# Second expert product: the last 64 tokens wholly from gathered rows, 192 dense tokens in five stationary sets

## The chip, the core and the metric

The kernel runs on one core of a Trainium2 chip. The metric is device time in microseconds; "before" is the median of three runs. TensorE (PE) multiplies matrices: a stationary operand of up to 128 columns is loaded (PEld), and a moving operand of up to 512 columns streams past it. VectorE (DVE), ScalarE (ACT) and GpSimd (POOL) work on 128 partitions; SyncE (SP) only starts DMA transfers here. Every engine takes its instructions in the order of the program; semaphores order the engines among each other.

## The reference

Two layers work on 256 tokens of 1024 numbers. Each layer first mixes tokens (convolution, windowed attention, spatial gating) and then runs PEER, a product-key retrieval over 16384 experts of one neuron each. Only PEER matters here:

```python
q = (t @ w_pq).reshape(T, PEER_HEADS, 2, PEER_HALF)
s = jnp.einsum('thpk,hpnk->thpn', q, sub_keys)
top_s, top_i = lax.top_k(s, PEER_TOPK)                 # 16 of 128 keys, twice per head
...
best_s, best_pos = lax.top_k(cand_s..., PEER_TOPK)     # 16 experts per head, 8 heads
gate = jax.nn.softmax(best_s, axis=-1)
act = jax.nn.gelu(einsum('td,thkd->thk', t, expert_down[experts]))
return einsum('thk,thkd->td', gate * act, expert_up[experts])
```

Each token so uses 128 of the 16384 experts. Scale and shift of the norms come from `c` by `w_ada`, 48 chunks of 128 outputs per layer ("modulation chunks").

## The kernel before

**First product.** `experts` computes the activations of all 16384 experts for all 256 tokens. The table `expert_down` comes in 128 chunks of 128 experts, 512 KB each, through five buffers `raw`. `cast_step` splits each chunk into a high half `hi` (ScalarE, L237) and a low half `lo` (VectorE, L230), with three buffers each, and `chunk_mm` makes 24 matmuls of 256 columns (8 row blocks by `hi x high`, `lo x high`, `hi x low`). GELU puts the result for a pair of chunks into `arena`.

**Gates.** `make_onehots` builds, for four tokens at a time, four one-hot matrices on GpSimd (L927) and three products on VectorE; `gate_mm` makes 8 small matmuls of them (L940, L941), whose result is the gate of every expert for these tokens. `gate_use` multiplies the activations of the chunks that are already there; `act_use` does it for later chunks. There are 64 such groups for 256 tokens; they are spread over the chunks from the end of the retrieval's work up to chunk 124 (`G_LAST`).

**Second product.** `combine` multiplies the gated activations, chunk by chunk, with `expert_up` (128 chunks of 128 experts by 1024 columns), under a hand-written order. `split(q)` makes high and low halves `hh` of four chunks' activations. A chunk has tokens 0 to 127 over 1024 columns and tokens 128 to 255 over `D - WIDE` columns, 768 in layer 0 and 640 in layer 1: 12 matmuls (L1037). Eight "whole" chunks per layer (`WHOLE_UP`) are multiplied unsplit in fp32; each of their matmuls runs as two.

**Gathered columns.** The last `WIDE` columns (256, 384) of the last 128 tokens come another way. During the first product SP copies these columns of `expert_up` into a DRAM tensor `rows`, and ScalarE's queue writes each pair's ungated activations of tokens 128 to 255 beside them. In the second product GpSimd gathers, for pick `k` of 128, one such row per token (token = partition) into a ring of eight buffers (`fetch`, L1017); VectorE takes the token's activation out of it by a product with the identity (L1023) and adds the weighted row to a sum (L1028, `add_row`). Row `k + 8` can be gathered when row `k` has been added. Rows are added between chunk 12 and chunk 125, about one per chunk, and each addition stands in VectorE's order between the low halves of the chunks, which run two chunks ahead.

**Modulation.** Layer 0's first product has 32 modulation chunks between its chunks, its second product 16, layer 1's first product 8. Each is a product with `c` and a sum on VectorE (L194), in two halves of 512 columns, with `c` in PSUM, in the first products.

At chunk 68 the second product loads `X` back from DRAM, and in layer 0 at chunk 72 `tables` loads three tables of the next layer by GpSimd's queue and masks one of them, for which GpSimd waits.

Of the kernel before, what the change touches and what calls it, by code (L numbers as in the profile page):

```python
# [9 lines left out]
F32 = mybir.dt.float32  # L10
# [7 lines left out]
P = 128  # L18
# [25 lines left out]
SPARSE = (True, True)  # L44
WIDE = (256, 384)
RING = 8
PICKS = 128
F_FIRST = 12
F_LAST = 125
WHOLE_UP = ((12, 24, 36, 48), (12, 24, 36, 48))  # L50
# [4 lines left out]
NG = S // 4  # L55
# [3 lines left out]
def hybrid_trunk(ctx: ExitStack, tc: tile.TileContext, x_in, c_in, vec_in, w_ada, w_in, w_out, w_pq,  # L59
# [34 lines left out]
    flat = arena.rearrange("p a b -> p (a b)")  # L94
    hh = consts.tile([P, 2, DC, S], F32R, name="hh")
    picks = consts.tile([P, S], F32, name="picks")
    parts = consts.tile([P, 3, S], F16, name="parts")
    chosen = consts.tile([P, 2, P], F32, name="chosen")
    c_dram = dram.tile([1, D], F32, name="c_dram")
    rows = {n: dram.tile([P * P, WIDE[n] + P], F32, name=f"rows{n}") for n in range(DEPTH) if SPARSE[n]}  # L100
# [38 lines left out]
    R_IX = region(0, 2, P)  # L139
    R_SUM = region(2 * S, max(WIDE))  # L140
# [22 lines left out]
    class Src:  # L163
        c = cact
# [24 lines left out]
    def ada_chunk(layer, col, raw):  # L189
        sides = Src.c if isinstance(Src.c, list) else [Src.c]  # L190
        w = D // len(sides)
        for k, (c, m) in enumerate(zip(sides, (mods[layer], halves))):
            v = raw[:, k * w:(k + 1) * w]
            op = nc.vector.scalar_tensor_tensor(v, v, 1.0, c, op0=OP.mult, op1=OP.mult, accum_out=m[:, col:col + 1])  # L194
            if len(sides) > 1 and k == 0:
                tc.keep_in_program_order(op)
        n = 8
        if layer == 0 and col < G1:
            n = 1
        if (col + 1) % n == 0:  # L200
            lo = col + 1 - n
            m = mods[layer][:, lo:lo + n]
            if len(sides) > 1:
                nc.vector.tensor_add(m, m, halves[:, lo:lo + n])
            nc.vector.tensor_add(m, m, vec[:, layer, V_ADA + lo:V_ADA + lo + n])
            if lo // 8 in (SC1 // 8, SC2 // 8):
                at = lo % 8 + (V_N1 if lo // 8 == SC1 // 8 else V_N2)
                nc.vector.scalar_tensor_tensor(m, m, 1.0, vec[:, layer, at:at + n], op0=OP.add, op1=OP.mult)

    def cast_step(late=None):  # L210
# [7 lines left out]
        if kind == "ada" and isinstance(Src.c, list):  # L218
# [5 lines left out]
        else:  # L224
# [20 lines left out]
            while Src.held:  # L245
                ada_chunk(*Src.held.pop(0))
# [12 lines left out]
    halves = consts.tile([P, 48], F32, name="halves")  # L259
    mods = [consts.tile([P, 48], F32, name=f"mod{i}") for i in range(DEPTH)]  # L260

    def ada(layer, groups):
        return [("ada", w_ada[layer, p], (layer, p)) for g in groups for p in range(8 * g, 8 * g + 8)]
# [15 lines left out]
    for layer in range(DEPTH):  # L279
# [16 lines left out]
        ups = [("whole" if n // 2 in WHOLE_UP[layer] else "mat", up[layer, n], None) for n in range(128)]  # L296
        if layer + 1 < DEPTH:
            dn = mix(dn, ada(0, [5]) + ada(1, range(3)), 24, 124)
            ups = mix(ups, ada(1, [3, 4]), 6, 120)
        else:  # L300
            dn = mix(dn, ada(1, [5]), 40, 120)
        seq += dn + ups
# [464 lines left out]
    def retrieval(layer, update, late):  # L767
# [80 lines left out]
        def to_picks(b):  # L848
# [4 lines left out]
            if b == 1 and SPARSE[layer]:  # L853
                nc.vector.scalar_tensor_tensor(chosen[:, 0, :], sel[:, 1, :], float(P), sel[:, 0, :], op0=OP.mult,
                                               op1=OP.add)
                nc.scalar.copy(chosen[:, 1, :], sel[:, 2, :])
            nc.vector.tensor_copy(picks[:, t], ps[:, 0:P])  # L857
# [57 lines left out]
    def experts(layer, rest):  # L915
# [28 lines left out]
        def gate_use(g, ps, done):  # L944
            v = ps.rearrange("p (t i) -> p i t", t=4)
            a = arena[:, :, 4 * g:4 * g + 4]
# [6 lines left out]
        def act(pair, ps, tdone):  # L953
            tmp = gelu(pair, ps, tdone)
            if SPARSE[layer]:
                i = 2 * pair
                ungated = work.tile([P, 2, P], F32, name="ungated", tag="ungated", bufs=1)
                nc.scalar.activation(ungated, ps.rearrange("p (i t) -> p i t", i=2)[:, :, P:], AF.Gelu)
                nc.scalar.dma_start(rows[layer].rearrange("(j i) c -> i j c", i=P)[:, i:i + 2, WIDE[layer]:], ungated)
                tc.keep_in_program_order(nc.sync.dma_start(  # L960
                    rows[layer][i * P:(i + 2) * P, :WIDE[layer]],
                    up[layer, i:i + 2, :, D - WIDE[layer]:].rearrange("j i c -> (j i) c")))
            return tmp

        def gelu(pair, ps, tdone):
            i = 2 * pair
            v = ps.rearrange("p (i t) -> p i t", i=2)
            if tdone < S:
                nc.scalar.activation(arena[:, i:i + 2, tdone:], v[:, :, tdone:], AF.Gelu)
            if tdone:  # L970
                tmp = work.tile([P, 2, S], F32, name="gt", tag="gt", bufs=1)
# [4 lines left out]
        def act_use(pair, tmp, tdone):  # L976
            if tmp is not None:
                i = 2 * pair
                a = arena[:, i:i + 2, :tdone]
                nc.vector.tensor_mul(a, a, tmp[:, :, :tdone])  # L980

        splits = {}

        def split(q):

            n = 2 if q == 0 or {2 * q, 2 * q + 1} & set(WHOLE_UP[layer]) else 4
            for i in range(4 * q, 4 * q + 4, n):
                src = arena[:, i:i + n, :]
                if i // 2 in WHOLE_UP[layer]:
                    hi, lo = src, None  # L990
                else:
                    slot = slice(i % 8, i % 8 + n)
                    hi, lo = hh[:, 0, slot, :S], hh[:, 1, slot, :S]
                    nc.scalar.copy(hi, src)
                    nc.vector.tensor_sub(lo, src, hi.bitcast(F32))  # L995
                for k in range(n):
                    splits[i + k] = hi[:, k, :], None if lo is None else lo[:, k, :]

        def combine(layer, late):


            qg = None
            sparse = SPARSE[layer]
            wide = WIDE[layer]
            dense = D - wide
            ring = region(4 * S, RING, wide + P)
            total = R_SUM[:, :wide]
            pieces = [(0, 0, 512), (0, 512, D)] + ([(1, 0, dense // 2), (1, dense // 2, dense)] if sparse else
                                                   [(1, 0, 512), (1, 512, D)])
            turns = [pieces[0], *pieces[2:], pieces[1]] if sparse else [pieces[0], pieces[2], pieces[1], pieces[3]]  # L1010
            acc = {p: bank("acc", 4) for p in turns}
            where, w8 = (R_IX[:, n, :] for n in range(2))
            fetched = added = 0

            def fetch(k):

                nc.gpsimd.indirect_dma_start(  # L1017
                    out=ring[:, k % RING, :], out_offset=None, in_=rows[layer][:, :],
                    in_offset=bass.IndirectOffsetOnAxis(ap=where[:, k:k + 1].bitcast(U32), axis=0))

            def add_row(k):
                v = ring[:, k % RING, :]
                nc.vector.scalar_tensor_tensor(v[:, wide:], v[:, wide:], chosen[:, 1, k:k + 1], ident, op0=OP.mult,  # L1023
                                               op1=OP.mult, accum_out=w8[:, k:k + 1])
                if k == 0:
                    nc.vector.tensor_scalar(total, v[:, :wide], w8[:, 0:1], None, op0=OP.mult)
                else:
                    nc.vector.scalar_tensor_tensor(total, v[:, :wide], w8[:, k:k + 1], total, op0=OP.mult, op1=OP.add)  # L1028

            if layer + 1 < DEPTH:  # L1030
                Src.c = work.tile([P, D], F32, name="cb", tag="oh", bufs=2)
                nc.gpsimd.dma_start(Src.c, bass.AP(tensor=c_dram.tensor, offset=c_dram.offset,
                                                   ap=[[0, P], [1, D]]))

            def add(i, piece, w, u, last=False):
                t, lo, hi = piece
                nc.tensor.matmul(acc[piece][:, :hi - lo], w[:, t * P:(t + 1) * P], u[:, lo:hi],  # L1037
# [224 lines left out]
```

## Time and profile before

| | |
|---|---|
| median of three runs | 1782.73 us (1777.23 to 1783.0) |
| profiled execution, its own time | 1781.52 us |
| its span in the trace | 1779.7 us |
| TensorE busy | 1728.6 us (97%) |
| VectorE busy | 1516.9 us (85%) |
| ScalarE busy | 916.7 us (52%) |
| GpSimd busy | 915.5 us (51%) |
| DMA | 493.36 MB, mean 277 GB/s |
| granted TensorE clock | 0.996 |

A layer's first product with its gates lies at about 205 to 594 us and 1085 to 1468 us, its second product at 594 to 912 and 1468 to 1774. The busy share of TensorE counts the modelled end of each matmul, which overlaps the next one; what TensorE really needs is seen from the distance of starts.

### The profile page before, as it was taken

Reading aid. Unit: us, or ns where it says so; the run is one execution under the profiler, and the core shown is the slowest. Engines: PE = TensorE matmul, PEld = TensorE weight load, DVE = VectorE, ACT = ScalarE, POOL = GpSimd, SP = SyncE. Lnnn points to the kernel's source line nnn. Section 1 sums busy time; section 2 is a strip of 40 time slices with the busy share of each in tenths; the row PEclk is TensorE's granted clock in tenths of the full one; section 3 lists DMA queues with packets and bytes.
Section 4 is the critical chain, followed back from the end, with each engine's and each line's share of the span. In section 5 each row is a group of like instructions: output and inputs, shape, how many; then the busy total and the mean of one; then the engine's idle time right before and its main releaser. Section 6 shows DMA issues by size and latency. Waiting matters only on the chain. (4 is left out here: it accounts for less than half of the span.)

```text
span 1779.7 us, 34446 instructions
## 1 busy us (share of the span) xinstructions
PE 1728.6 (97%) x12504; PEld 1595.0 (90%) x12504; DVE 1516.9 (85%) x3465; ACT 916.7 (52%) x1421; POOL 915.5 (51%) x827
## 2 busy tenths in 40 slices
PE   7999999999999999999999999999999999999998
PEld 6889999999999888888889899999999998888886
DVE  5868997789889689989987599958888878999998
ACT  2446455555445544444557565655555455444553
POOL 1000203679989267666600002128999964777672
PEclk9999999999999999999999999999999999999999
DMA  9965688888878899999964447988887778999995
GB/s 365 320 236 177 206 254 301 279 278 273 280 251 266 287 325 328 332 363 323 352 202 143 169 151 237 295 272 264 270 263 259 257 255 294 358 349 347 348 357 204
DMA packets 190011, 493.36 MB, mean 277 GB/s; under 512 B 19537, under 2 KB 85457, under 8 KB 188690
## 3 DMA queue, kind: packets, MB, share of 16 engines
q1 hardware_dynamic: 134752, 405.33, 67.3%
q0 software_dynamic: 20128, 68.96, 10.6%
q10 hardware_dynamic: 34962, 16.88, 3.2%
q8 instruction: 98, 1.61, 0.4%
q14 instruction: 71, 0.58, 0.1%
HBM read 471.16 MB, written 61.87 MB: 300 GB/s over the span
## 5 line engine op out<-in xcount | busy, mean ns | idle before, releaser
L237 ACT CAST hi<-raw 128x1024 fp32r<-128x1024 f32 x538 | 564.5, 1051 | 594.5 <-PE ch L314 242.2
L230 DVE TENSOR_TENSOR lo<-raw,hi 128x1024 fp32r<-128x1024 f32 x538 | 660.0, 1228 | 115.5 <-ACT hi L237 111.7
L313 PE MATMUL ch<-hh,lo 128*128 128x256 f32 x2336 | 652.9, 279 | 7.5 <-DVE lo L230 7.5
L312 PE MATMUL ch<-hh,hi 128*128 128x256 f32 x2336 | 658.2, 282 | 0.0
L314 PE MATMUL ch<-hh,hi 128*128 128x256 f32 x2336 | 649.9, 278 | 0.0
L927 POOL TENSOR_SCALAR oh<-iota,picks 128x128 f16<-128x128 f16 x512 | 502.6, 1000 | 212.2 <-DVE picks L857 105.1
L1017 POOL DMA_INDIRECT arena<-rows,arena x256 | 373.5, 1459 | 222.9 <-DVE arena L1028 111.8
L313 PEld LDWEIGHTS ch<-hh,lo 128*128 128x128 f32 x2336 | 441.4, 189 | 9.6 <-DVE lo L230 9.1
L312 PEld LDWEIGHTS ch<-hh,hi 128*128 128x128 f32 x2336 | 441.0, 189 | 0.3 <-issue 0.3
L314 PEld LDWEIGHTS ch<-hh,hi 128*128 128x128 f32 x2336 | 440.0, 188 | 0.0
L1037 PE MATMUL acc<-hi,hh 128*128 128x512 f32 (+2 forms) x1920 | 420.7, 360 | 5.4 <-DVE hh L995 2.7
L1037 PEld LDWEIGHTS acc<-hi,hh 128*128 128x128 f32 x1920 | 339.9, 188 | 52.6 <-DVE hh L995 7.0
L1037 PE MATMUL acc<-lo,hh 128*128 128x512 f32 x960 | 231.4, 361 | 2.9 <-DVE lo L230 2.8
L1037 PEld LDWEIGHTS acc<-lo,hh 128*128 128x128 f32 x960 | 173.1, 188 | 28.3 <-DVE lo L230 5.4
L1028 DVE SCALAR_TENSOR_TENSOR arena<-arena 128x256 f32<-128x256 f32 (+1 forms) x254 | 140.3, 552 | 9.1
L932 DVE TENSOR_TENSOR oh<-oh,parts 128x512 f16<-128x512 f16 x256 | 101.6, 439 | 0.0
L788 POOL CAST arena<-arena 128x512 f16<-128x512 uint32 x32 | 27.2, 865 | 141.7 <-DVE arena L777 113.2
L951 ACT ACTIVATE arena<-g 128x240 f32<-128x240 f32 (+35 forms) x128 | 41.5, 325 | 100.0 <-DVE arena L948 91.5
L194 DVE SCALAR_TENSOR_TENSOR raw<-raw,acc 128x512 f32<-128x512 f32 x80 | 54.4, 680 | 43.8 <-DMA raw<-in_w_ada 43.7
L1023 DVE SCALAR_TENSOR_TENSOR arena<-arena,chosen,ident 128x128 f32<-128x128 f32 x256 | 88.8, 347 | 0.0
L940 PE MATMUL g<-oh 128*128 128x128 f16 x512 | 74.8, 222 | 10.5 <-POOL oh L927 6.9
L752 POOL DMA_DIRECT2D arena<-in_keys x2 | 1.2, 578 | 150.1 <-issue 96.8
(233 smaller groups left out, 1840.5 us busy)
## 6 DMA issues: line engine op xcount, KB each, us to landing
raw<-in_down SPq DMA_DIRECT2D x256, 512.0 KB, 4.7
raw<-in_up SPq DMA_DIRECT2D x256, 512.0 KB, 5.3
raw<-in_w_ada SPq DMA_DIRECT2D x96, 512.0 KB, 4.8
rows<-in_up SPq DMA_DIRECT2D x64, 384.0 KB, 5.7
raw<-in_w_pq SPq DMA_DIRECT2D x32, 512.0 KB, 4.0
rows<-in_up SPq DMA_DIRECT2D x64, 256.0 KB, 5.4
rows<-ungated ACTq DMA_DIRECT2D x128, 128.0 KB, 4.7
raw<-in_w_in SPq DMA_DIRECT2D x26, 512.0 KB, 4.5
```

The lines of the kernel that those rows point to most:

```text
L230: nc.vector.tensor_sub(lo, raw, hi.bitcast(F32))
L237: nc.scalar.copy(hi, raw)
L312: nc.tensor.matmul(dst, hi[:, cols], k[0], start=start, stop=False, **kw)
L313: nc.tensor.matmul(dst, lo[:, cols], k[0], start=False, stop=False, **kw)
L314: nc.tensor.matmul(dst, hi[:, cols], k[1], start=False, stop=stop, **kw)
L927: nc.gpsimd.tensor_scalar(oh[:, i, :], iota, picks[:, t:t + 1], None, op0=OP.is_equal)
L932: nc.vector.tensor_tensor(og[j], on, wide(1 + j), op=OP.mult)
L940: nc.tensor.matmul(dst, oh[:, i, :], og[0][:, i // 2, :, i % 2], start=True, stop=False)
L1017: nc.gpsimd.indirect_dma_start(out=ring[:, k % RING, :], out_offset=None, in_=rows[layer][:, :], in_offset=bass.IndirectOffsetOnAxis(ap=wh ...
L1023: nc.vector.scalar_tensor_tensor(v[:, wide:], v[:, wide:], chosen[:, 1, k:k + 1], ident, op0=OP.mult, op1=OP.mult, accum_out=w8[:, k:k + 1])
L1028: nc.vector.scalar_tensor_tensor(total, v[:, :wide], w8[:, k:k + 1], total, op0=OP.mult, op1=OP.add)
L1037: nc.tensor.matmul(acc[piece][:, :hi - lo], w[:, t * P:(t + 1) * P], u[:, lo:hi], start=piece not in opened, stop=last, skip_group_check=True)
```

## The change

The first 192 tokens are now dense over all 1024 columns, and the last 64 come wholly from gathered rows.

- `T = 192`: the gates are made for 192 tokens, in 48 groups (`NG`). `acts` is the arena with 192 tokens per chunk.
- `split` keeps high and low halves of 192 tokens in `sides`, and a second copy of the high half of tokens 128 to 191 behind their low half. So one stationary set `w1` holds 64 low and 64 high columns. A chunk has five stationary uses: `w0h` and `w0l` with `uh`, `w1` with `uh`, `w0h` and `w1` with `ul`, each over two pieces of 512 columns, 10 matmuls. `fold` (two identities one above the other) adds the two halves at the end, in `turn`.
- No chunk of `expert_up` is whole any more: 16 more chunks are split by `cast_step`.
- For the last 64 tokens a partition stands for a token and half of its picks: `pairs` holds 64 picks for each of 128 partitions. `fetch` gathers rows of 1024 columns from `expert_up` itself, 64 per layer, into a ring of four. Nothing is copied to `rows` any more; only the ungated activations of 64 tokens go to `act_rows`, and they are gathered apart, 64 gathers of 64 columns, in groups of eight (`fetch_acts`). `weights` takes a group's activations out by `fold`, three VectorE instructions. Group `g + 2` uses the buffers of group `g` and is gathered after `weights(g)`.
- Layer 0's first product has all 48 modulation chunks, each as one product of 1024 columns with `c` in SBUF; the second product has none.
- Additions run from chunk 9 to 126; `X` is loaded at chunk 92, the tables at 84.

```diff
+T = 192
+TS = S - T
+RING = 4
+GROUP = 8
+F_FIRST = 9
+F_LAST = 126
...
+                nc.scalar.copy(hi, src)
+                nc.scalar.copy(slot[:, :, 2 * T:2 * T + TS], src[:, :, P:])
+                nc.vector.tensor_sub(lo, src, hi.bitcast(F32))
...
+            def fetch_acts(g):
...
+                for k in range(g * GROUP, (g + 1) * GROUP):
+                    nc.gpsimd.indirect_dma_start(
+                        out=R_ACTS[:, k % (2 * GROUP), :], out_offset=None, in_=act_rows[layer][:, :],
+                        in_offset=bass.IndirectOffsetOnAxis(ap=where_act[:, k:k + 1].bitcast(U32), axis=0))
...
+                nc.vector.tensor_tensor(v, v, fold[:, None, :].to_broadcast([P, GROUP, TS]), op=OP.mult)
+                nc.vector.tensor_reduce(w, v, op=OP.add, axis=AX.X)
+                nc.vector.tensor_mul(w, w, pairs[:, 1, g * GROUP:(g + 1) * GROUP])
...
+            while fetched < RING:
+                fetch(fetched)
+                fetched += 1
+            fetch_acts(0)
+            fetch_acts(1)
             for i in range(128):
                 if i % 4 == 2 and 4 < i < 124:
                     split(i // 4 + 1)
                 uh, ul = next_chunk()
...
+                while added < want(i):
+                    add_row(added)
+                    added += 1
+                    if fetched < TS:
+                        fetch(fetched)
                         fetched += 1
+                g = -(-want(i + 2) // GROUP) - 1
+                if i >= F_FIRST - 2 and g > -(-want(i + 1) // GROUP) - 1:
+                    weights(g)
+                    if 1 < g + 2 < TS // GROUP:
+                        fetch_acts(g + 2)
...
+                    for w in (w0h, w0l):
+                        for p in pieces[:2]:
+                            add(i, p, w, uh)
+                    for p in pieces[2:]:
+                        add(i, p, w1, uh)
                     for p in pieces:
+                        add(i, p, w1 if p[0] else w0h, ul)
```

GpSimd's order in the second product of layer 0, before (L1017 are the rows, L1078 is `X`, L462 to L467 are the tables):

```order
L927 TENSOR_SCALAR oh<-iota,picks 128x128 x256
L1032 DMA cb<-c_dram 128x1024
L1117 DMA cb<-c_dram 128x1024
L1017 DMA arena<-rows_99,arena 128x384 x73
L1078 DMA arena<-x_dram 128x2048
L1017 DMA arena<-rows_99,arena 128x384 x5
L462 DMA arena<-in_rel_bias 128x2048
```

and of the change (L1006 are rows of 1024 columns, L1013 the activations):

```order
L925 TENSOR_SCALAR oh<-iota,picks 128x128 x192
L1006 DMA arena<-in_up,arena 128x1024 x4
L1013 DMA arena<-act_rows_102,arena 128x64 x24
L1006 DMA arena<-in_up,arena 128x1024 x8
L1013 DMA arena<-act_rows_102,arena 128x64 x8
L1006 DMA arena<-in_up,arena 128x1024 x8
```

Three groups of activations now stand between row four and row five, and eight gathers ahead of every eight rows after that. Further on, the tables follow two rows behind the last group:

```order
L1013 DMA arena<-act_rows_102,arena 128x64 x8
L1006 DMA arena<-in_up,arena 128x1024 x2
L458 DMA arena<-in_rel_bias 128x2048
L459 DMA arena<-in_sgu_w 128x512
L460 DMA arena<-in_sgu_b 128x256
L461 AFFINE_SELECT arena<-arena 128x512
L463 MEMSET arena 128x2x2
L1006 DMA arena<-in_up,arena 128x1024 x4
```

VectorE's order at the first additions of layer 0, before (L230 are low halves, L194 a modulation chunk, L995 a split):

```order
L194 SCALAR_TENSOR_TENSOR raw,mod_108<-raw,cb 128x1024
L230 TENSOR_TENSOR lo<-raw,hi 128x1024
L1023 SCALAR_TENSOR_TENSOR arena<-arena,chosen,ident 128x128
L1026 TENSOR_SCALAR arena<-arena 128x256
L1023 SCALAR_TENSOR_TENSOR arena<-arena,chosen,ident 128x128
L1028 SCALAR_TENSOR_TENSOR arena<-arena 128x256
L230 TENSOR_TENSOR lo<-raw,hi 128x1024
L1023 SCALAR_TENSOR_TENSOR arena<-arena,chosen,ident 128x128
L1028 SCALAR_TENSOR_TENSOR arena<-arena 128x256
L995 TENSOR_TENSOR hh<-arena,hh 128x1024
```

and of the change (L229 are low halves, L1021 to L1023 the weights of a group, L1028 the first and L1030 every later addition, L989 a split):

```order
L229 TENSOR_TENSOR lo<-raw,hi 128x1024 x2
L1021 TENSOR_TENSOR arena<-arena,fold 128x512
L1022 TENSOR_REDUCE arena<-arena 128x8
L1023 TENSOR_TENSOR arena<-arena,pairs 128x8
L229 TENSOR_TENSOR lo<-raw,hi 128x1024 x2
L1028 TENSOR_SCALAR arena<-arena 128x1024
L989 TENSOR_TENSOR hh<-arena,hh 128x4x192
L229 TENSOR_TENSOR lo<-raw,hi 128x1024
L1030 SCALAR_TENSOR_TENSOR arena<-arena 128x1024
L229 TENSOR_TENSOR lo<-raw,hi 128x1024 x2
```

The weights of the first group stand ahead of the low halves of chunks 10 and 11, and one addition in 1.8 chunks takes the place of two instructions in 0.9.

## Rows read from the trace of the kernel before

**Rows 1.** Busy time of each engine (with instructions) in four stretches.

```profile
330.00:575.00 245.00, 238.19 (x2247) 233.87 (x2246) 219.25 (x446) 125.54 (x245) 214.16 (x230) 0.99 0.84 271
594.00:912.00 318.00, 315.71 (x1497) 271.41 (x1498) 289.34 (x575) 155.82 (x156) 184.56 (x134) 0.99 0.92 324
1205.00:1450.00 245.00, 239.50 (x2273) 235.00 (x2272) 206.47 (x385) 128.54 (x249) 235.64 (x232) 1.00 0.81 261
1468.00:1774.00 306.00, 301.65 (x1519) 252.76 (x1517) 286.53 (x543) 152.88 (x153) 192.49 (x129) 1.00 0.90 325
```

In rows 1 the columns after the stretch are its length, then PE, PEld, DVE, ACT and POOL busy, the granted clock, DMA share and GB/s.

**Rows 2.** TensorE in order of time, first product: start, duration, line, operation.

```profile
483.43 0.23 PE L940 MATMUL g<-oh 128*128 128x128 f16 x1
...
484.33 0.36 PE L312 MATMUL ch<-hh,hi 128*128 128x256 f32 x1
...
590.89 0.28 PE L312 MATMUL ch<-hh,hi 128*128 128x256 f32 x1
...
592.02 0.28 PE L313 MATMUL ch<-hh,lo 128*128 128x256 f32 x1
```

**Rows 3.** Gate matmuls by line, 1205 to 1450 us: busy, mean, idle before, releaser.

```profile
L940 PE MATMUL g<-oh 128*128 128x128 f16 x236 | 34.3, 222 | 4.6 <-POOL oh L927 4.4
```

**Rows 4.** TensorE in order of time, second product of both layers.

```profile
594.47 0.73 PE L1037 MATMUL acc<-hi,hh 128*128 128x512 f32 x2 [2.05 <-ACT hh L994]
...
621.23 0.62 PE L1037 MATMUL acc<-hi,hh 128*128 128x512 f32 x2
621.23 0.85 PE L1037 MATMUL acc<-hi,hh 128*128 128x512 f32 x3
...
773.63 6.18 PE L1037 MATMUL acc<-raw,arena 128*128 128x512 f32 x16
...
782.07 1.77 PE L1037 MATMUL acc<-hi,hh 128*128 128x512 f32 x8
...
784.49 1.77 PE L1037 MATMUL acc<-hi,hh 128*128 128x512 f32 x8
...
1522.75 5.75 PE L1037 MATMUL acc<-raw,arena 128*128 128x512 f32 x16
...
1530.61 1.67 PE L1037 MATMUL acc<-hi,hh 128*128 128x512 f32 x8
...
1532.88 1.67 PE L1037 MATMUL acc<-hi,hh 128*128 128x512 f32 x8
```

**Rows 5.** VectorE in order of time, second product of layer 1.

```profile
1497.85 0.35 DVE L1023 SCALAR_TENSOR_TENSOR arena<-arena,chosen,ident 128x128 f32<-128x128 f32 x1
...
1498.24 0.62 DVE L1028 SCALAR_TENSOR_TENSOR arena<-arena 128x384 f32<-128x384 f32 x1
1498.78 1.22 DVE L230 TENSOR_TENSOR lo<-raw,hi 128x1024 fp32r<-128x1024 f32 x1
1499.91 0.35 DVE L1023 SCALAR_TENSOR_TENSOR arena<-arena,chosen,ident 128x128 f32<-128x128 f32 x1
```

**Rows 6.** Groups of instructions over the span, shapes apart.

```profile
L1017 POOL DMA_INDIRECT arena<-rows,arena x256 | 373.5, 1459 | 222.9 <-DVE arena L1028 111.8 <-DVE lo L230 40.6 <-DVE hh L995 30.2
...
L194 DVE SCALAR_TENSOR_TENSOR raw<-raw,arena 128x1024 f32<-128x1024 f32 x40 | 48.5, 1218 | 16.6 <-DMA raw<-in_w_ada 9.0 <-ACT arena L367 3.6 <-PE g L519 2.5
```

**Rows 7.** GpSimd in order of time; in brackets the idle time before and its releaser.

```profile
615.61 0.95 POOL L1017 DMA_INDIRECT arena<-rows,arena  x1 [0.30 <-issue]
...
777.77 0.59 POOL L462 DMA_DIRECT2D arena<-in_rel_bias  x1
...
788.92 1.00 POOL L1017 DMA_INDIRECT arena<-rows,arena  x1 [0.16 <-issue]
...
1506.38 1.76 POOL L1017 DMA_INDIRECT arena<-rows,arena  x1 [0.30 <-issue]
```

**Rows 8.** DMA issues of GpSimd's queue: count, KB each, median us to landing.

```profile
arena<-rows,arena POOLq DMA_INDIRECT x256, 6.2
...
cb<-c_dram POOLq DMA_DIRECT2D x2, 512.0 KB, 8.6
```

More of the change, by code (lines that the diff above doesn't have):

```diff
@@ L187, in run_fill, with ada_chunk @@
             Src.credit -= cost
[L189 to L196, printed above, removed]
+    def ada_chunk(layer, col, raw, held=False):
+        op = nc.vector.scalar_tensor_tensor(raw, raw, 1.0, cact, op0=OP.mult, op1=OP.mult,
+                                            accum_out=mods[layer][:, col:col + 1])
+        if held:
+            tc.keep_in_program_order(op)
         n = 8
@@ L217, in cast_step @@
         Src.cast += 1
[L218 removed]
+        if kind == "held":
             Src.held.append((arg[0], arg[1], raw))
@@ L257, in next_chunk, with ada @@
         return ready.popleft()
-    halves = consts.tile([P, 48], F32, name="halves")
     mods = [consts.tile([P, 48], F32, name=f"mod{i}") for i in range(DEPTH)]
-    def ada(layer, groups):
-        return [("ada", w_ada[layer, p], (layer, p)) for g in groups for p in range(8 * g, 8 * g + 8)]
+    def ada(layer, groups, kind="ada"):
+        return [(kind, w_ada[layer, p], (layer, p)) for g in groups for p in range(8 * g, 8 * g + 8)]
     def mix(a, b, first=0, last=None):
@@ L852, in to_picks @@
             t = slice(b * P, (b + 1) * P)
-            if b == 1 and SPARSE[layer]:
+            if b == 1:
                 nc.vector.scalar_tensor_tensor(chosen[:, 0, :], sel[:, 1, :], float(P), sel[:, 0, :], op0=OP.mult,
@@ L954, in act @@
             tmp = gelu(pair, ps, tdone)
[L955 to L962, printed above, removed]
+            i = 2 * pair
+            ungated = work.tile([P, 2, TS], F32, name="ungated", tag="ungated", bufs=2)
+            nc.scalar.activation(ungated, ps.rearrange("p (i t) -> p i t", i=2)[:, :, T:], AF.Gelu)
+            nc.scalar.dma_start(act_rows[layer].rearrange("(j i) c -> i j c", i=P)[:, i:i + 2, :], ungated)
             return tmp
@@ L1010, in combine @@
-            turns = [pieces[0], *pieces[2:], pieces[1]] if sparse else [pieces[0], pieces[2], pieces[1], pieces[3]]
+            pieces = [(t, lo, lo + 512) for t in range(2) for lo in (0, 512)]
+            turns = [pieces[0], pieces[2], pieces[1], pieces[3]]
             acc = {p: bank("acc", 4) for p in turns}
-            where, w8 = (R_IX[:, n, :] for n in range(2))
+            rows = up.rearrange("l j i c -> (l j i) c")
+            where_act, where_row, w8 = (R_IX[:, n, :] for n in range(3))
@@ L1035, in add @@
             def add(i, piece, w, u, last=False):
                 t, lo, hi = piece
-                nc.tensor.matmul(acc[piece][:, :hi - lo], w[:, t * P:(t + 1) * P], u[:, lo:hi],
-                                 start=piece not in opened, stop=last, skip_group_check=True)
+                nc.tensor.matmul(acc[piece], w, u[:, lo:hi], start=piece not in opened, stop=last,
+                                 skip_group_check=True)
                 opened.add(piece)
@@ L1105, in combine @@
             high = [bank("acc", 4) for _ in range(2)]
[L1106 to L1120 removed]
+            turn(1, 0, high)
+            turn(1, 1, high)
+            return low + high, qg
         gdone = 0
```

156 lines of the change are left out of this document (60 added, 96 removed).

## Prediction

> **What bounds the kernel now.** I read the stages first [rows 1]. Of the 1779.7 us, two stretches per layer matter. In the first product with gates (330 to 575 us, 1205 to 1450 us) TensorE is busy 97 to 98%, GpSimd 87 and 96%, VectorE 89 and 84%. In the second product (594 to 912, 1468 to 1774) TensorE is busy 99%, VectorE 91 and 94%, and DMA has a share of 0.90 to 0.92. "Busy" counts a matmul's modelled end too, so I counted work against cadence. In the first product 10 matmuls start between 590.89 and 592.02 us, 0.113 us each [rows 2], so a chunk of 24 is 2.72 us; 16 gate matmuls start between 483.43 and 484.33, so a gate group of 8 is 0.45 us. The stretch from 330 us holds 230/4 = 57.5 groups (four one-hots each) and (2247 - 460)/24 = 74.5 chunks: 202.6 + 25.9 = 228.5 of 245 us, so 16.5 us are waits. From 1205 us: 58 groups, 75.4 chunks, 231.2 of 245, 13.8 us of waits. Of the waits ahead of the gate matmuls in layer 1 nearly all end with a one-hot of GpSimd [rows 3].
>
> In the second product one 512-column matmul follows the last by 0.23 us (two end after 0.62, three after 0.85 us) [rows 4]. An ordinary chunk is 784.49 - 782.07 = 2.42 us in layer 0 and 1532.88 - 1530.61 = 2.27 in layer 1. Two whole chunks and one ordinary lie between 773.63 and 782.07, so a whole chunk is (8.44 - 2.42)/2 = 3.01 us; in layer 1 (7.86 - 2.27)/2 = 2.79. With 120 ordinary and 8 whole chunks TensorE needs 290.4 + 24.1 = 314.5 of 318 us in layer 0, so 3.5 us of waits, and 272.4 + 22.3 = 294.7 of 306 in layer 1, so 11.3 us. VectorE explains the difference: a low half takes 1498.78 to 1499.91, 1.13 us, a row 1497.85 to 1498.78, 0.93 us [rows 5]. Per chunk of layer 1 that is 1.13 + 128/113 x 0.93 + a quarter of a split of 1.13 = 2.46 us, over TensorE's 2.27.
>
> **The change, part by part.** *Gates.* 48 groups per layer in place of 64: 32 x 0.45 = **-14.4 us** of TensorE, in a stretch that it bounds. GpSimd makes 384 one-hots in place of 512, VectorE a quarter fewer products. So the 30.3 us of waits in the two stretches shrink; none of them must go, all can. Against it, layer 0 has 48 modulation chunks in its first product, not 32. I take half, as GpSimd falls from 96% to about 72% busy, VectorE only slightly: **-15** (0 to -30).
>
> *TensorE in the second product.* Every chunk is now 10 matmuls of 512 columns, 10 x 0.231 = 2.31 us, 295.7 us per layer. Layer 0: 120 x (2.42 - 2.31) + 8 x (3.01 - 2.31) = 18.8 off; layer 1: 120 x 0.04 more, 8 x 0.48 off, +1.0. Together **-17.8**. The folding matmuls at the end (16 of 64 columns for 8 transposes, per layer) are an exposed microsecond or less each: **+1.5**.
>
> *VectorE in the second product.* A row of 1024 columns stands in no row; the same form on 1024 columns takes 1.218 us [rows 6], and I take 1.2. There are 64, so 0.55 per chunk. A chunk costs 1.13 + 0.66 + a quarter of a split of 0.9 + the weights, two passes of 512 columns and a short one, 1.35 us once per 14.6 chunks: 2.1 us, under 2.31. So the throughput wait of layer 1 goes: **-10** of the 14.8 us of both layers (-3 to -13; the 2.05 us at the start of layer 0 [rows 4] remain). The 16 more casts lie on ScalarE, 156 us busy of 318 [rows 1], and in VectorE's sum above: nothing.
>
> *GpSimd's queue.* There are still 128 gathers per layer, but in another order: 4 rows, 24 gathers of 64 columns, then row number five. Before, nothing stood between rows, and eight were buffered; now four are. A gather with its pause takes 0.95 + 0.30 = 1.25 us at best and 1.76 + 0.30 = 2.06 at worst [rows 7]; the mean of 256 is 1.46 + 0.30 = 1.76 [rows 6]. Early in the product VectorE is less loaded; I take 1.65. Landing took 6.2 us from issue for rows of 192 to 256 KB, 8.6 for 512 KB from the same queue [rows 8]; a row is now 512 KB, and I take 7, nearer the gathers because the 8.6 us piece spreads one row over all partitions.
>
> The walk, from the product's first matmul: VectorE computes the weights of the first eight picks in iteration 7, behind the low half of chunk 9, at 7 x 2.31 + 1.13 = 17 us. The twelfth gather is out at 18 to 20 and lands at about 26. VectorE stands still, and behind it in its order stand all later low halves. TensorE has chunks up to 9 and the high half's matmuls of chunk 10, until 24.5; the low half of 10 is there at 26 + 1.35 + 1.13 = 28.5. That is about 4 us. Then row five: VectorE reaches it in iteration 16, at 38 + 4 = 42 us; 12 gathers were out at 20, 13 more by 42, the last 3 at 1.25 follow, and the row's own gather lands 7 us later, at 52 to 53. With the addition, a split and a low half (1.2 + 0.9 + 1.13) chunk 19 can go on at 56; TensorE has work until 19 x 2.31 + 1.4 + 4 = 49. So 4 + 7 = 11, less some overlap: 10 us per layer, **+20** (0 to +34: at 1.25 both come in time, at 2.06 and 8.6 us I get 17 per layer).
>
> After that, five bursts of eight gathers per layer stand ahead of a row. From the weights at iteration 21: 1.35 + 8 x 1.76 + 7 = 22.4 us, while the row is wanted at iteration 30, 9 x 2.31 = 20.8 later. So it is 1.6 us late. TensorE has three prepared chunks and loses nothing until about 4 us; VectorE wins back 14.6 x 0.2 = 3 us between bursts. I take 1 us a burst, **+10** (0 to +20). The tables of the next layer hold the queue for 788.92 - 777.77 = 11.2 us [rows 7]; now right behind the last burst: 1.3 + 14.1 + two rows of 1.76 + 11.2 + 7 = 37 us, for row 46, wanted 13 iterations (30 us) after those weights. 7 late, less what the cushion has left: **+5** (2 to 10), layer 0 alone.
>
> *Sum:* -14.4 - 15 - 17.8 + 1.5 - 10 + 20 + 10 + 5 = -20.7. 1779.7 - 20.7 = 1759, and 1781.5 was measured around a span of 1779.7, so **1761 us**; the profiled execution lies 1.2 us under the median of the three runs, so the median would be 1762. I call it 1761.
>
> On the gathers a rule of the Trainium skill speaks against this change. The rows [rows 7] show 0.95 and 1.76 us for the same instruction. The page "SBUF — State Buffer", section "SBUF: two separate sides", says that VectorE and GpSimd share a port pair as an exclusive lock, that whoever starts first holds it for the whole instruction, and that descriptors which GpSimd writes for a DMA wait for it. By that, long VectorE instructions one behind the other (1.2 us in place of pieces of 0.35 to 0.6) would put every gather at the 2.06 us end, and the sum at the second rival's 1791; by the mean row it is 1761. No row has 1024-column additions beside gathers, so I leave its weight to that rival.
>
> **The rivals.** *Gathers hidden.* If a gather stays near 1.25 us and lands in 5 to 6, the four rows and the cushion of three chunks cover everything; the second product runs at 2.31 us a chunk: 1761 - 35 = **1726**. For it: VectorE has fewer instructions. Against it: 28 gathers in a row were never seen at 1.25.
>
> *Gathers set the pace; the other side.* At 2.06 us and 8.6 us to landing: 17 per layer at the start (34), a burst is late by 1.35 + 16.5 + 8.6 - 20.8 = 5.6 us of which 3.5 are won back, 2.1 x 10 = 21, tables 10: 65 us in place of 35, **1791**. Each further microsecond to landing costs 1 per burst and start, some 13 us. For it: the product moves 192 pieces of 0.52 MB and 2.1 MB, 102.8 MB, in 296 us, 347 GB/s, where [rows 1] show 324 at a share of 0.92; at a share of 1 the 103 MB of layer 0 need 0.92 x 318 = 293 us, so DMA does not become the bound but hardly leaves room. It decides slower from 35 + 21 + 5 = 61 us of new waits on.
>
> *No relief in the first product.* If the waits there stay (low halves wait on modulation chunks, or the scheduler puts the gates elsewhere), only the 14.4 us go: **1776**. For it: TensorE's waits for low halves do not come from the gates.
>
> **How the numbers follow.** Forecast 0.50 (1742 to 1775), gathers hidden 0.17, no relief 0.15, gathers set the pace 0.18. A difference of 0.3%, 5 us, is about what the runs can tell. Faster: 0.50 + 0.17 + a third of 0.15 = 0.72. Same: 0.10 + 0.02 = 0.12. Slower: 0.16. The range that leaves out about a tenth on either side reaches into both gather cases: 1728 to 1794.
>
> **What would show it.** Right: in the second product 2.31 us per chunk of ten; VectorE's two longest idle pieces per layer ended by DMA, on the weights of the first group and on row five; GpSimd under 80% in the first product's gated stretch. Wrong: rows of 1024 columns well over 1.3 us, so that VectorE is the bound again; row landings over 9 us; GpSimd one-hots still releasing gate matmuls; waits of ScalarE for raw chunks that reach TensorE.

## The result and the profile after

| | before | changed |
|---|---|---|
| median | 1782.19 us | 1808.18 us |
| lowest to highest | 1777.23 to 1783.0 | 1800.96 to 1808.87 |
| span of the profiled execution | 1779.7 us | 1806.6 us |
| mean granted clock there | 0.996 | 0.987 |

The ratio is 1.0143 with a 95% interval of 1.0111 to 1.0174. The kernel became 26 us slower; forecast were 1761 us, in a range of 1728 to 1794, and 1808 lies above it.

First the same four stretches as in [rows 1], of the changed kernel (length, then PE, PEld, DVE, ACT and POOL busy, granted clock, DMA share, GB/s).

```profile
330.00:575.00 245.00, 245.00 (x2229) 243.28 (x2228) 215.25 (x373) 119.36 (x239) 208.60 (x174) 1.00 0.80 258
594.00:912.00 318.00, 293.12 (x1211) 233.96 (x1210) 254.19 (x240) 159.25 (x183) 193.96 (x128) 0.96 0.90 318
1205.00:1450.00 245.00, 245.00 (x2235) 243.37 (x2234) 183.19 (x315) 119.65 (x240) 178.38 (x180) 1.00 0.62 196
1468.00:1774.00 306.00, 283.71 (x1187) 226.64 (x1186) 248.01 (x238) 157.08 (x183) 201.13 (x129) 0.97 0.89 320
```

In the first product TensorE is now busy in all 245.00 us of both stretches, and GpSimd fell from 235.64 to 178.38 us in layer 1: the waits went, and more of them than foreseen. But counted as the prediction counts, the 174 one-hots of the first row are 43.5 gate groups, 348 matmuls and 19.6 us; the other 1881 matmuls took 225.4 us, 0.120 each, where the forecast had 0.113. In the second product TensorE stood for 25 and 22 us, and the granted clock is 0.96 and 0.97.

The cadence, which is the step from the start of one matmul to the start of the next, shows the same directly. TensorE in order of time, as in [rows 2] (start, duration, line, operation); nine matmuls start between the two rows, one every 0.119 us instead of 0.113.

```profile
450.08 0.28 PE L310 MATMUL ch<-hh,hi 128*128 128x256 f32 x1
...
451.15 0.28 PE L310 MATMUL ch<-hh,hi 128*128 128x256 f32 x1
```

Over 330 to 550 us the mean step from one 256-column matmul to the next was 114.4 ns before (113.3 in most chunks, 117.8 in the others) and is 118.6 ns now, in every chunk. No instruction of these matmuls was changed, and the granted clock of the stretch is 1.00.

In the second product VectorE's waits show what is late. Its waits by what it waited for (total, times, longest), the first two lines of layer 0 (from 580 us on), the third of layer 1 (from 1468 us on):

```profile
DVE arena L1030 <- DMA arena<-in_up,arena: 39.7, 6, 7.5
...
DVE arena L1021 <- DMA arena<-act_rows,arena: 6.1, 1, 6.1
...
DVE arena L1030 <- DMA arena<-in_up,arena: 39.8, 7, 8.5
```

L1030 adds a gathered row, so 13 waits for rows cost VectorE 79.5 us. One of them from the weights of its group (L1021) on, GpSimd and VectorE together in order of time; what stands in brackets is the idle time before and its releaser:

```profile
683.59 0.69 DVE L1021 TENSOR_TENSOR arena<-arena,fold 128x512 f32<-128x512 f32 x1
...
685.39 1.80 POOL L1013 DMA_INDIRECT arena<-act_rows,arena  x1 [0.30 <-DVE arena L1023]
...
691.75 1.32 DVE L1030 SCALAR_TENSOR_TENSOR arena<-arena 128x1024 f32<-128x1024 f32 x1
691.82 0.94 POOL L1013 DMA_INDIRECT arena<-act_rows,arena  x1 [0.30 <-issue]
...
698.59 0.95 POOL L1013 DMA_INDIRECT arena<-act_rows,arena  x1 [0.30 <-issue]
...
699.76 2.35 DVE L229 TENSOR_TENSOR lo<-raw,hi 128x1024 fp32r<-128x1024 f32 x2
699.84 1.96 POOL L1006 DMA_INDIRECT arena<-in_up,arena  x1 [0.30 <-DVE arena L1030]
...
709.62 1.28 DVE L1030 SCALAR_TENSOR_TENSOR arena<-arena 128x1024 f32<-128x1024 f32 x1 [7.50 <-DMA arena<-in_up,arena]
...
711.83 0.80 PE L1034 MATMUL acc<-hi,hh 128*128 128x512 f32 x1 [4.16 <-DVE hh L989]
```

The eight small gathers (L1013) hold the queue from 685.39 to 699.54. Only then goes the gather of the row (L1006), and it is there at 709.62, 26.0 us after the weights began. VectorE had come to that row at 702.1, 18.5 us after them. Behind the row stand a split (L989) and the next low halves, and TensorE, with three chunks prepared, stops for 4.16 us.

A stop can cost more than itself. The windows ahead of this stop, after it and after that (length, busy times, granted clock, DMA share, GB/s):

```profile
700.00:707.20 7.20, 7.20 (x32) 5.83 (x32) 2.12 (x2) 4.42 (x6) 4.61 (x4) 1.00 0.90 280
...
711.80:715.00 3.20, 3.17 (x8) 2.52 (x9) 3.20 (x3) 1.06 (x2) 0.78 (x1) 0.51 0.64 177
715.00:720.00 5.00, 5.00 (x23) 4.07 (x22) 5.00 (x6) 2.97 (x4) 2.70 (x2) 1.00 0.94 334
```

For 3.2 us after the stop TensorE runs at half speed, 1.2 in place of 2.4 GHz: a 512-column matmul every 0.427 us instead of 0.232. Over both second products the time beyond the ordinary step (0.2324 us here, each kernel's own further down) adds up to 67.7 us: 49.5 in 15 stops, 15.9 in 77 matmuls at the lower clock behind them, the rest in small ones. Five of the 15 stops, of 1.3 to 2.9 us, have no slow matmul behind them. The forecast had 35.

One piece of the 67.7 us is not a late row. Around 624 to 635 us, at the start of layer 0, TensorE lost 8.0 us; VectorE stood there 5.09 and 3.31 us ahead of two low halves (L229), for which the profile names no releaser, and took row five at 634.75 us without a wait. What held it stays open; run d below has no such stop.

### The profile page after: what moved, and what is told of

Same layout as the page of the kernel before. It is cut to its first block, busy times and chain, and to the rows that moved or that the text cites. A ratio compares the mean times of both kernels' runs of the same rounds, so it can differ in the third digit from the quotient of the medians.

```text
span 1806.6 us, 32055 instructions
## 1 busy us (share of the span) xinstructions
PE 1734.2 (96%) x11848; PEld 1578.5 (87%) x11848; DVE 1433.9 (79%) x2679; ACT 905.6 (50%) x1469; POOL 870.6 (48%) x697
## 4 chain that ended last, share of the span: by engine, by line
PE 76%; DVE 9%; issue 5%; DMA 4%; POOL 4%; ACT 1%; SPq 0%; DVEq 0%; POOLq 0%; ACTq 0%
PE acc L1034 22%; PE ch L308 14%; PE ch L309 14%; PE ch L310 14%; POOL arena L1013 3%; DVE lo L229 3%; PE ch L306 2%; DMA arena<-in_up,arena 2%; PE g L938 1%; PE g L939 1%; PE ch L388 1%; DMA raw<-in_w_ada 1%; PE acc L308 1%; PE acc L310 1%; PE acc L309 1%
## 5 line engine op out<-in xcount | busy, mean ns | idle before, releaser
L229 DVE TENSOR_TENSOR lo<-raw,hi 128x1024 fp32r<-128x1024 f32 x554 | 676.4, 1230 | 154.2 <-ACT hi L236 138.5
L925 POOL TENSOR_SCALAR oh<-iota,picks 128x128 f16<-128x128 f16 x384 | 429.8, 1136 | 258.1 <-issue 148.3
L1034 PE MATMUL acc<-hi,hh 128*128 128x512 f32 x1536 | 411.6, 403 | 19.3 <-DVE hh L989 17.0
L1034 PEld LDWEIGHTS acc<-hi,hh 128*128 128x128 f32 x1536 | 295.4, 193 | 91.8 <-DVE hh L989 19.2
L1034 PE MATMUL acc<-lo,hh 128*128 128x512 f32 x1024 | 288.5, 403 | 27.9 <-DVE lo L229 27.9
L1006 POOL DMA_INDIRECT arena<-in_up,arena x128 | 193.2, 1509 | 199.6 <-DVE arena L1030 126.7
L1030 DVE SCALAR_TENSOR_TENSOR arena<-arena 128x1024 f32<-128x1024 f32 x126 | 161.6, 1283 | 79.5 <-DMA arena<-in_up,arena 79.5
L1013 POOL DMA_INDIRECT arena<-act_rows,arena x128 | 204.3, 1596 | 40.6 <-issue 33.5
L194 DVE SCALAR_TENSOR_TENSOR raw<-raw,arena 128x1024 f32<-128x1024 f32 x96 | 117.2, 1223 | 16.6 <-DMA raw<-in_w_ada 10.7
L928 DVE TENSOR_TENSOR oh<-iota,parts 128x512 f16<-128x512 f16 x96 | 41.5, 434 | 35.5 <-PE g L939 29.5
L989 DVE TENSOR_TENSOR hh<-arena,hh 128x768 fp32r<-128x768 f32 (+1 forms) x66 | 61.3, 929 | 0.6 <-ACT hh L987 0.3
```

The source lines that it names most:

```text
L194: op = nc.vector.scalar_tensor_tensor(raw, raw, 1.0, cact, op0=OP.mult, op1=OP.mult, accum_out=mods[layer][:, col:col + 1])
L229: nc.vector.tensor_sub(lo, raw, hi.bitcast(F32))
L925: nc.gpsimd.tensor_scalar(oh[:, i, :], iota, picks[:, t:t + 1], None, op0=OP.is_equal)
L1006: nc.gpsimd.indirect_dma_start(out=R_ROWS[:, k % RING, :], out_offset=None, in_=rows, in_offset=bass.IndirectOffsetOnAxis(ap=where_row[:, ...
L1013: nc.gpsimd.indirect_dma_start(out=R_ACTS[:, k % (2 * GROUP), :], out_offset=None, in_=act_rows[layer][:, :], in_offset=bass.IndirectOffse ...
L1030: nc.vector.scalar_tensor_tensor(R_SUM, v, w8[:, k:k + 1], R_SUM, op0=OP.mult, op1=OP.add)
```

## The experiments

Two theories came out of this. *Queue:* the 67.7 us come from rows that stand behind bursts of eight small gathers on GpSimd's queue. *Placement:* the slower cadence of the first product comes from where the two new tiles of constants pushed the streamed chunks. All of a group ran on one chip beside the kernel before; a ratio is to that one.

**a and b, placement alone.** The change put `pairs` and `fold` (768 bytes per partition) into the pool of constants and took a tile of 192 out, so everything allocated behind them, `raw`, `hi` and `lo` first, lies 576 bytes further. Run a adds an unused tile, run b gives the kernel before the same 576 bytes:

```diff
 fold = consts.tile([P, TS], F32, name="fold")
 nc.vector.tensor_add(fold, ident[:, :TS], ident[:, TS:])
+pad = consts.tile([P, 112], F32, name="pad")
+nc.vector.memset(pad, 0.0)
```

> The changed kernel with one unused tile of 448 bytes per partition behind the new tiles of constants, so that the streamed chunks (raw, hi, lo) lie 1024 bytes per partition further than in the kernel before, at the same offset within 1024 bytes, instead of 576 bytes further. No instruction of the products changes. Theory placement (the slower cadence of 256-column matmuls comes from where the two new tiles pushed the chunks): cadence back from 118.6 ns to 113 to 115 in most chunks; 3072 such matmuls per layer in the first product and some 1100 elsewhere times 4 to 5 ns, so 30 us less: about 1775 us. Rival traffic (it comes from other engines' new reads and writes): cadence stays at 118.6, 1808 us. Rival instruction stream (the order or number of instructions ahead): also 1808.

Measured: 1785.08 us (ten runs), ratio 1.0017 (0.9996 to 1.0037); 23 us less than the changed kernel. In its TensorE order of time ten matmuls take 1.13 us:

```profile
412.00 0.28 PE L311 MATMUL ch<-hh,lo 128*128 128x256 f32 x1
...
413.13 0.28 PE L312 MATMUL ch<-hh,hi 128*128 128x256 f32 x1
```

The mean step is 113.9 ns. The gain is 10 us less than expected, and the second products account for some 7 of them: with the 512-column matmuls at 228.9 ns instead of 232.4, their stops and slow matmuls grew from 67.7 to 75 us.

> The kernel before with one unused tile of 576 bytes per partition ahead of its modulation tiles, so that its chunks lie where those of the changed kernel do. Theory placement: cadence of 256-column matmuls from 113.3 (with stretches at 117.8) to 118.6 ns all along; less is lost than the matmuls add, as part of it lies in the waits of the first product: 20 to 35 us slower, 1802 to 1817. Rivals traffic and instruction stream: within 5 us of 1782.

Measured: 1797.39 us, ratio 1.0093 (1.0059 to 1.0127), 16 us slower, mean step 118.6 ns, nine matmuls in 1.07 us:

```profile
410.07 0.28 PE L315 MATMUL ch<-hh,lo 128*128 128x256 f32 x1
...
411.14 0.28 PE L315 MATMUL ch<-hh,lo 128*128 128x256 f32 x1
```

So 576 bytes that nothing reads slow the old kernel down. That it is 16 and not 20 or more fits the waits of the kernel before: part of the slower matmuls lies where TensorE waited, and its idle time in the first and third stretch of [rows 1] fell from 12.3 to 4.7 us. Theories *traffic* and *instruction stream* are out.

**c and d, the queue alone.** Run c spreads the small gathers, run d makes them bursts of four (`GROUP = 4` in place of 8, and nothing else).

```diff
+fetch_acts(0, GROUP)
 while fetched < RING:
     fetch(fetched)
     fetched += 1
-fetch_acts(0)
-fetch_acts(1)
...
 add_row(added)
 added += 1
...
 fetch(fetched)
 fetched += 1
+at = GROUP + min(added - 1, GROUP) + added - 1
+fetch_acts(at, at + (2 if added <= GROUP else 1))
...
 weights(g)
-if 1 < g + 2 < TS // GROUP:
-    fetch_acts(g + 2)
```

> The changed kernel with the gathers of 64 columns no longer in bursts of eight: those of the first group ahead of the four first rows, then two behind each of the first eight rows and one behind each later row. Theory queue (the new waits come from rows that stand behind a burst on GpSimd's queue): the waits of VectorE's additions on DMA fall from 79.5 us to under 15, the excess over 2.31 us a chunk in the second product from 68 us to 20 to 30: 1762 to 1772 us. Rival landing (a row needs longer to land than four rows of buffer last, whatever stands ahead of it): waits spread over all rows, a sum of 60 us or more, 1800 to 1812. Rival VectorE (it is the bound, waits only move): 1800.

Measured: 1754.93 us, ratio 0.9861 (0.9827 to 0.9896), so 53 us less, beyond the 1762 to 1772 expected. VectorE's waits for rows, first in layer 0:

```profile
DVE arena L1030 <- DMA arena<-in_up,arena: 15.4, 7, 3.9
```

and 7.9 us in layer 1, 23.3 in place of 79.5; more than the 15 expected, but most are short enough for TensorE's three prepared chunks. The time beyond its ordinary step fell from 67.7 to 12.9 us.

> The changed kernel with bursts of four gathers of 64 columns in place of eight (twice as many, eight at the start in place of sixteen). Theory queue: a burst holds the queue 5 to 7 us less, so a row of each burst is late by 0 to 1 us in place of 3 to 4, and row five is in time; 35 to 50 us of waits go, against 8 more weight steps per layer of about 0.6 us on VectorE that its slack takes: 1765 to 1778 us. Rivals landing and VectorE: 1800 to 1815.

Measured: 1743.02 us, ratio 0.9781 (0.9753 to 0.9808), so 65 us less, beyond the best end. Layer 0 of VectorE's waits and the windows of both second products:

```profile
DVE arena L1030 <- DMA arena<-in_up,arena: 4.8, 2, 4.4
```

```profile
582.00:885.00 303.00, 300.75 (x1301) 242.25 (x1299) 270.08 (x277) 170.73 (x199) 183.22 (x134) 1.00 0.94 349
...
1435.00:1734.00 299.00, 299.00 (x1299) 242.78 (x1298) 267.97 (x274) 166.39 (x193) 185.45 (x129) 1.00 0.91 338
```

The time beyond the ordinary step is 3.4 us in all, and the granted clock is 1.00: with the stops the slow matmuls behind them go too. *Queue* holds; *landing* and *VectorE* are out. VectorE does the same additions as before (and eight weight steps more per layer), and the rows land from the same memory.

**e, both.**

> The changed kernel with bursts of four (run d_group4) and with the 448 bytes that put the chunks back to the offset of before (run a_pad448). If the two causes are apart and add up: 256-column cadence 113 to 115 ns, 512-column 229, no pause of TensorE over 2 us in the second product, granted clock 1.00; 1743 - 23 = 1720, with 3 ns more off each of 2560 512-column matmuls now that nothing else sets the pace there: 1710 to 1726. If the faster products bring the waits back (VectorE has less room at 2.29 us a chunk): 1728 to 1740.

Measured: 1714.18 us, ratio 0.9608 (0.9584 to 0.9632). The causes add up, 29 us off d: by the traces 6.7 of them in the second products (595.9 us in place of 602.6), the rest outside them. This kernel is 94 us under the changed one and 71 under the one before.

**f to o, what it is about the place.** All have bursts of four; only the bytes and where they stand differ. f, g, h, l, n and o have the tile of run a with 64, 32, 224, 384, 480 and 416 bytes; m has 64 bytes ahead of `hh` besides the 448. The edits of i, j and k, one behind the other:

```diff
+pad = consts.tile([P, 112], F32, name="pad")
 hh = consts.tile([P, 2, DC, S], F32R, name="hh")
...
 dma_ahead(RAW)
+pad = stream.tile([P, 112], F32, name="pad")
...
+pairs = consts.tile([P, 2, TS], F32, name="pairs")
 hh = consts.tile([P, 2, DC, S], F32R, name="hh")
...
-pairs = consts.tile([P, 2, TS], F32, name="pairs")
```

> Bursts of four and 64 bytes in place of 448: the chunks lie at the offset of before within 128 bytes (96), at another one within 512 and 1024. If the offset within 128 bytes is what counts: cadence 113.3, 1720. If a wider one counts: 118.6, 1743.

> Bursts of four and 32 bytes: the chunks begin at a multiple of 64 bytes, which they did neither before nor after the change (both 32 beyond one). If rows that begin on such a multiple are read faster: cadence under 113 ns, 1705 to 1718. If only the offset of before helps: 118.6, 1743.

> Bursts of four and 224 bytes: the chunks begin at a multiple of 512 bytes, the size of one row of a stationary set. If a multiple of that counts: cadence under 113 ns, at or below run g_g4_pad32 by over 5 us. If a multiple of 64 is enough: the same as g_g4_pad32 within 5 us. If only the offset of before helps: 118.6, 1743.

> Bursts of four, and the 448 bytes ahead of hh (the activations that move through the 256-column matmuls) in place of behind it: the chunks lie at the offset of before (736 of 1024), hh 448 further, so that the distance from hh to the chunks is that of the changed kernel. If the chunks' own offset counts: cadence 113.3, 1714 as e_g4_pad448. If the distance between what is loaded as weights and what moves counts: 118.6, 1743.

> Bursts of four, and the 448 bytes between raw and hi: hi and lo, which TensorE reads, lie at the offset of before, raw, which it reads in the whole chunks only, where the changed kernel has it. If TensorE's own reads count: cadence 113.3, about 1714. If it is the traffic to raw (DMA, ScalarE, VectorE) that disturbs it: 118.6, 1743.

> Bursts of four, no tile added, but the new tile pairs (512 bytes) allocated ahead of hh: the chunks stay at the offset of the changed kernel (288), hh moves to 160 of 1024; the distance from hh to the chunks becomes 128 within 1024, where before had 64 and the changed kernel 640. If the chunks' own offset counts: 118.6, 1743. If the distance counts: another cadence, 113 or so if any small distance is good (1714), near 118 if 64 is special.

> Bursts of four and 384 bytes behind hh: the distance from hh to the chunks is a multiple of 1024, the chunks' offset 672. If the distance counts and a small one is good: 113 ns or less, 1714 or less. If chunks and hh at the same offset are in each other's way: over 118.6 ns, over 1743. If only the offset of before helps: 1738 to 1757, as the other three.

> Bursts of four, 64 bytes ahead of hh and 448 behind it: hh at 736 of 1024, the chunks at 800, so that the distance of before (64 within 1024) is kept and both offsets are others. If the distance decides: cadence 113 to 114 with stretches at 117.8, 1714 to 1717. If the pair of offsets of before decides: 118 or more, 1738 to 1757.

> Bursts of four and 480 bytes behind hh: a distance of 96 within 1024. If the neighbourhood of 64 is fast: a cadence between 113 and 117, 1710 to 1730. If the value alone is: 117 to 120, 1738 to 1757, as the distances 0, 128, 640, 672, 704 and 864.

> Bursts of four and 416 bytes behind hh: a distance of 32 within 1024. As n_g4_pad480: 113 to 117 ns and 1710 to 1730 if the neighbourhood is fast, 117 to 120 ns and 1738 to 1757 if the value alone is.

Offsets, as the programs allocate the tiles, are within 1024 bytes of a partition; the step is the mean of 256-column matmuls from 330 to 550 us in the one profiled execution of each, the last columns the mean step of 512-column matmuls and the median of the runs. The distance is that of the first product, where `hi` and `lo` are the stationary sets and `hh` moves. In the second product of the changed kernels the roles are swapped, and the stationary sets begin 0, 768 and 1280 bytes into a slot of `hh`, so that the column does not give the distances there.

| run | hh | hi, lo | distance | 256 cols, ns | 512 cols, ns | us |
|---|---|---|---|---|---|---|
| before | 672 | 736 | 64 | 114.4 | 231.2 | 1782 |
| d | 672 | 288 | 640 | 118.6 | 232.3 | 1743.0 |
| e | 672 | 736 | 64 | 114.0 | 228.8 | 1714.2 |
| f | 672 | 352 | 704 | 117.7 | 233.3 | 1738.0 |
| g | 672 | 320 | 672 | 119.9 | 234.2 | 1756.5 |
| h | 672 | 512 | 864 | 118.6 | 233.2 | 1742.8 |
| i | 96 | 736 | 640 | 118.6 | 232.3 | 1742.6 |
| j | 672 | 736 (raw 288) | 64 | 114.0 | 228.9 | 1716.8 |
| k | 160 | 288 | 128 | 118.6 | 232.3 | 1741.4 |
| l | 672 | 672 | 0 | 119.7 | 226.7 | 1740.4 |
| m | 736 | 800 | 64 | 113.9 | 228.8 | 1715.9 |
| n | 672 | 768 | 96 | 118.6 | 233.3 | 1741.3 |
| o | 672 | 704 | 32 | 118.3 | 233.2 | 1741.0 |

i and m decide. In i the chunks lie where they do in e, and TensorE is slow, since hh moved with them; in m both lie elsewhere and it is fast, since their distance is that of before, ten matmuls in 1.13 us:

```profile
410.02 0.28 PE L312 MATMUL ch<-hh,hi 128*128 128x256 f32 x1
...
411.15 0.28 PE L313 MATMUL ch<-hh,lo 128*128 128x256 f32 x1
```

j shows that it is hi and lo, not raw, that count beside hh. ScalarE and VectorE write hi and lo, but these writes are not it: in the changed kernel the step is 118.7 ns while neither writes, 118.3 while ScalarE does and 118.7 while VectorE does (in the kernel before 114.5, 114.7 and 114.3). That leaves TensorE's own two reads: the set that is loaded as weights and the columns that move past it. A multiple of 64 or 512 bytes (g, h) does not help, nor the offset of before within 128 bytes (f), nor a neighbour (n, o). Of nine distances one is fast, 64, with the actual distance 1024 longer in a, e, j and m than in before. Why that one, the runs do not tell, and whether 256 or 512 further would do was not tried.

## Why the prediction was wrong

The terms of its sum, with what the profiled executions and the runs show. The relief is what remains of run a's gain outside the second products (38.4 us) beside the gates; the cadence is the difference between a and the changed kernel there. Both rest on one profiled execution each.

| term | forecast | measured |
|---|---|---|
| gates | -14.4 | -14.4 (32 groups fewer; a gate matmul's step is 58 ns in both) |
| relief in the first product | -15 | -24 |
| cadence of 256-column matmuls | not in the sum | +23 |
| TensorE in the second products, throughput wait of VectorE | -17.8 - 10 | -27 |
| start of the gathers, both layers | +20 | +23.8 |
| ten bursts | +10 | +38.7 |
| tables of layer 0 | +5 | +4.9 |
| end, with the folds | +1.5 | +1.8 |
| sum | -20.7 | +26.9 of span |

**Right.** A chunk of ten matmuls costs 2.32 us (2.31 forecast). A second product is 336.8 and 330.3 us, less 37.1 and 30.6 of stops and slow matmuls 299.7 in both, where it took 321.2 and 305.2 before. The gate matmuls' waits for GpSimd went (4.6 us of idle time ahead of them in [rows 3], 0.0 now). The tables cost what they were priced at. The start of the gathers cost about 11.8 us in either layer, near the forecast, but only layer 1 went as walked through (2.5 us at the weights of the first group, then row five with 8.47 us of waiting on VectorE); in layer 0 the larger part is the 8.0 us that no row explains. That the sum of both layers fits is in part luck, and the sign that was named for it, VectorE's two longest idle pieces on the first weights and on row five, held for row five of layer 1 alone.

**Mis-sized: "I take 1 us a burst, +10".** It was 3.9 us a burst, for three reasons. First the gathers: from the first to the last of eight, the ten bursts took 14.1 to 20.7 us, 17.2 on average, or 2.2 us for each gather with its pause, where the sum had 1.76. That is the condition of the rival in which the gathers set the pace (2.06), and its 65 us of waits are close to the 67.7, though partly by luck: it had 34 of them at the starts and 21 in the bursts, where 23.8 and 38.7 were measured. Second, VectorE came to the row 18.8 us after the weights on average (25.1 until the row was used, less 6.35 idle), not 20.8: the walk let it go at TensorE's 2.31 us a chunk, but from the weights on it works at its own pace, and at the prediction's own 2.1 us a chunk nine chunks are 18.9. So it is there early and finds no row. The landing was priced too high rather (6.1 us from issue to use over the twelve late rows, 7 in the sum). With the row late by 6.3 us on VectorE and not 1.6, TensorE's cushion was used up in nine of the ten bursts. Third, the sum priced a stop by its length alone; 15.9 us went with the lower clock behind the stops, which run d gave back with them.

What goes with the slow gathers is seen in a later burst, of layer 1, again both engines in order of time:

```profile
1651.85 1.27 DVE L1030 SCALAR_TENSOR_TENSOR arena<-arena 128x1024 f32<-128x1024 f32 x1
1653.05 0.95 DVE L989 TENSOR_TENSOR hh<-arena,hh 128x768 fp32r<-128x768 f32 x1
1653.06 4.03 POOL L1013 DMA_INDIRECT arena<-act_rows,arena  x1 [0.30 <-issue]
1653.92 2.35 DVE L229 TENSOR_TENSOR lo<-raw,hi 128x1024 fp32r<-128x1024 f32 x2
1656.19 1.27 DVE L1030 SCALAR_TENSOR_TENSOR arena<-arena 128x1024 f32<-128x1024 f32 x1
...
1661.72 1.22 DVE L229 TENSOR_TENSOR lo<-raw,hi 128x1024 fp32r<-128x1024 f32 x1
1664.06 0.94 POOL L1013 DMA_INDIRECT arena<-act_rows,arena  x1 [0.30 <-issue]
1665.31 0.94 POOL L1013 DMA_INDIRECT arena<-act_rows,arena  x1 [0.30 <-issue]
```

While VectorE's instructions follow one another without a gap, a gather takes up to 4.03 us; once VectorE stands and waits for the row, every gather takes 0.94. Over both second products the 59 gathers during which VectorE stood took 0.93 to 1.02 us each, and the 160 during which it worked throughout 1.7 us on average, though a fifth of these were under 1 us too. The load of the DMA engines does not explain it: their share was 0.90 during the burst of 685 us and 0.92 when VectorE stood behind it. That VectorE's work is the cause is read from this coincidence; no run changed it alone. The Trainium skill, page "SBUF — State Buffer", section "SBUF: two separate sides", has the port pair that VectorE and GpSimd share as an exclusive lock for a whole instruction. The trace agrees that busy VectorE and slow gathers go together, with 0.94 against 4.03 us, but not that every gather is blocked: 23 lie as a whole inside one VectorE instruction and took under 1 us, as the one at 691.82 us inside the addition from 691.75 on. The prediction left the rule's weight to the rival at 2.06 us a gather; the mean of the bursts lay above that.

**Missing: the cadence.** The sum had nothing for it: it took 0.113 us per matmul for granted, as no matmul of the first product was changed, and 0.119 was measured, 23 us. Two small tiles in a pool of constants moved its operands. Without this the changed kernel would still not have been faster (run a, 1.0017); without the bursts' waits it would have been faster in spite of it (run d, 0.9781). Rival "no relief" fell. "Gathers hidden", 1726, comes near what the change is worth without the bursts' waits and the slower cadence: e has 1714, and 9 of the 12 us between them are the relief, 24 in place of 15.

## What to carry to other kernels

Adding or dropping a tile moved every later tile of the pools here: before reading a slower matmul as contention, compare the start-to-start step of an untouched matmul in both traces, and if it changed, try padding that restores the old distance between its two operands (no other amount brought the old step back here). On a queue that works in order, count what stands ahead of the one transfer that somebody waits for, with the durations of the busy state and the consumer at its own fastest pace; bursts of four in place of eight were worth 65 us here. A stop of TensorE costs its length and, behind ten of the 15 stops here, slower matmuls too, which a sum of waits leaves out.

## What the runs showed of the hardware

- The step of 256-column matmuls was 113.9 to 114.4 ns at one distance between weights and moving columns in SBUF (64 within 1024 bytes of a partition) and 117.7 to 119.9 ns at eight others; that of 512-column matmuls, whose operands lie at other distances, between 226.7 and 234.2 ns in the same kernels, with its best value in run l.
- Within one kernel the step has two levels that hold for whole chunks: 113.3 and 117.8 ns before, the lower in most.
- In the changed kernel a gather took 0.93 to 1.02 us of GpSimd with VectorE idle (59 of them), and 1.7 on average, 4.03 at most, with VectorE busy throughout (160); the share of the DMA engines was about the same in both.
- After a stop of 4.16 us TensorE's granted clock was 0.51 (1.2 GHz) for the next 3.2 us; the second products of run d, whose stops are under 1 us, show 1.00.
